# Attention probabilities scaled on GpSimd instead of VectorE and ScalarE, and six low-part splits moved the other way

## The chip, the core and the metric

The kernel runs on one core of one Trainium2 chip. A core has several engines with their own instruction streams: TensorE (PE in the profile; its weight loads are listed apart as PEld), VectorE (DVE), ScalarE (ACT), GpSimd (POOL) and SyncE (SP), which here issues loads. The engines work on SBUF, a memory of 128 partitions; matrix products land in PSUM banks and are read from there by VectorE and ScalarE. Each engine works through its own instructions in order and waits on semaphores for the others. DMAs are issued from the streams of SyncE and GpSimd, so an issue stands in line with that engine's other instructions.

The metric is the device time of one execution in microseconds. The kernel before took 1936.27 us, the median of three runs from 1935.07 to 1936.42.

## The reference

One layer of an encoder trunk over 1024 tokens of width 1024, all in float32:

```
h = x + 1/2 * SwiGLU_1(RMSNorm(x))
[qA|kA|vA|qB|kB|vB|gA|gB] = RMSNorm(h) @ W_in
yA = NeighbourhoodAttention2D(qA, kA, vA)      # 8 heads of 64, learned 2-D bias
yB = WindowedGQA(rope(qB), rope(kB), vB)       # 8 heads, 2 key heads, window 128, sink logit
h = h + (sigmoid(gA) * (yA @ W_A) + sigmoid(gB) * (yB @ W_B)) @ W_out
h = h + 1/2 * SwiGLU_2(RMSNorm(h))
y = RMSNorm(h)
```

The attention B has one learned sink logit for each head. It joins the denominator of the softmax without a value:

```
m = max(max(s), sink)
e = exp(s - m)
p = e / (sum(e) + exp(sink - m))
```

## The kernel before

**Precision.** Matrix products are taken with operands split in two: a high part, which is a copy rounded to the format `fp32r`, and a low part, the difference. The helper `split` does it: line 93 copies on ScalarE, line 94 subtracts on VectorE or on the engine given to it. A product then takes three passes, lines 145, 147 and 149 of the helper `mm3`. So L93, L94, L145, L147 and L149 in the profile belong to many callers, told apart by the tile (`ws` weights and probabilities, `ar` large resident operands, `fx` values, `raw` what a load brought).

**Stages.** First feed-forward, input projection, attention with the gate projections between, the branch products and the merge, second feed-forward, final norm. The change touches the attention stage alone, roughly 846 to 1118 us of the span.

**Units.** Attention is cut in 64 units. A unit is one block of 128 queries for two heads (s = 0, 1). Units 0 to 31 belong to attention B (8 query blocks, 4 head pairs each), units 32 to 63 to attention A (4 head pairs, 8 query blocks each). The first and last query block see two key blocks (256 columns), the others three (384 columns).

A unit passes three functions, each in a later turn of one loop:

- `scores(un)`: for each head, two matmuls into a PSUM bank `d` (L1278, L1279). For units of attention B a copy of the sink logit into column 0 of the tile's row (L1282). A fused instruction on VectorE adds the bias and finds the minimum of the negated scores, `nmx` (L1283). ScalarE takes the exponential and its sum, `ssum` (L1286). After both heads VectorE takes the reciprocals `rc` of the two sums (L1289) and scales head 0 (L1290); ScalarE scales head 1 (L1291). The probabilities lie in `fa`, in two buffers used in turn; `fa` also holds biases and the outputs of attention A.
- `turn(un)`: the probabilities are transposed by TensorE into PSUM (L1299) and split (L93 on ScalarE, L94 on VectorE) into `ws`.
- `values(un)`: products with the values (L1313, L1318), whose result goes to the output blocks (L1231, L1233, L1252, L1253, L1256) and from there to memory by a store from GpSimd's queue.

**The loop.** Turn n issues scores(n), then a step of filler work, turn(n−1), another step, values(n−2). The filler is a generator of matmul groups that do not depend on the units: the gate projections (L145, L147, L149 into `g`), at the end of the stage the products of branch B. At n = 23, 33, 41 and 49 `prep_a` prepares the next head pair of attention A: twelve loads issued from GpSimd (L1090, L1092), one more load, transposes of the values (L1104), and their splits into `fx`.

**Outputs y.** When the outputs of attention are complete they are read back from memory and split for the branch products: `split_y`, called for four blocks of B (two in the last gate step, two at the head of `branch_b`) and for three blocks of A (at n = 60, 61, 62). Six of the seven calls give GpSimd for the low part (L94, `ar` from `raw`, 128 x 1024); one of B's gives VectorE.

**What sets the order.** The program is written in the order above; a list scheduler then sets each engine's own order from the dependences and from when it expects results to be ready. A longer expected time on one engine can so move other instructions within TensorE's order.

Of the kernel before, what the change touches and what calls it, by code (L numbers as in the profile page):

```python
# [12 lines left out]
AF = mybir.ActivationFunctionType  # L13
ALU = mybir.AluOpType

P = 128
# [20 lines left out]
def trunk_kernel(ctx, tc, x, xt, n1, wg1, wu1, wd1, nm, win, rpb, sink, wa, wb, wo,  # L37
                 n2, wg2, wu2, wd2, nf, c_rope, c_mask_a, c_mask_b, out):
    nc = tc.nc
# [33 lines left out]
    def new_ar(g, dt=F32R):  # L73
        ar[g] = main.tile([P, 4, 1024], dt, tag=f"ar{g}", bufs=1, name=nm_("ar"))
        return ar[g]

    def slot(k):
        return ar[k // 4][:, k % 4, :]

    def bank(tag):  # L80
        return ps.tile([P, 512], F32, tag=tag, name=nm_(tag))
# [10 lines left out]
    def split(dst_hi, dst_lo, src, eng=None):  # L92
        nc.scalar.copy(dst_hi, src)  # L93
        (eng or nc.vector).tensor_tensor(dst_lo, src, f32v(dst_hi), op=ALU.subtract)  # L94
# [12 lines left out]
    def load_w(w, c0, r=None, eng=None):  # L107

        return load_split(ws4(), ws4(), w_cols(w, c0), w.shape[0] // P, P, r, eng)
# [41 lines left out]
    def drain(gen, n=1 << 30):  # L151

        for _ in range(n):
            if next(gen, gen) is gen:
                return
# [784 lines left out]
    def by_block(a):  # L940

        return a.rearrange("p (b j x) -> p j b x", b=NTT, x=16)

    def in_block(a):
        return a.rearrange("p (j b x) -> p j b x", b=NTT, x=16)
# [170 lines left out]
    def gate(dc, steps):  # L1116

        w = mix.pop("gate")
        bs = [bank("g"), bank("g")]
        for k, c in enumerate((4, 5, 6, 7, 0, 1, 2, 3)):  # L1120
            mm3(bs, k == 0, k == NC8 - 1, (w[0][:, c, :], w[1][:, c, :]), [u_half(c, n) for n in range(2)])
            yield
            if k in steps:
                steps[k]()
        gt = xs4()
        for n in range(2):
            nc.scalar.copy(gt[:, n * 512:(n + 1) * 512], bs[n])
        nc.gpsimd.dma_start(g_d[dc * P:(dc + 1) * P, :], gt)
# [5 lines left out]
    def branch_w(w, dc, eng=None, r=None):  # L1134

        t = ws4()
        if r is None:
            r = fetch_branch(raw4()[:, :512], w, dc)
        split(t[:, :512], t[:, 512:], r, eng)
        return [t[:, k:k + 512].rearrange("p (c f) -> p c f", f=P) for k in (0, 512)]  # L1140

    Y_A, Y_B = ((12, 13), (14, 15), (20, 21), (22, 23)), ((4, 5), (6, 7), (0, 1), (2, 3))

    def branch_mm(bs, w, y):

        for c in range(4):
            mm3(bs, c == 0, c == 3, (w[0][:, c, :], w[1][:, c, :]),
                [[slot(k)[:, n * 512:(n + 1) * 512] for k in y[c]] for n in range(2)])
            yield

    def fetch_y(r0):
        mix["y", r0] = raw4()
        nc.sync.dma_start(mix["y", r0], y_d[r0:r0 + P, :])

    def split_y(slots, r0, eng):

        h, l = [slot(k) for k in slots]
        r = mix.pop(("y", r0))
        if r0 < 512:
            r = in_block(r)  # L1160
            h, l = by_block(h), by_block(l)
        split(h, l, r, eng)
# [4 lines left out]
    def branch_a(i):  # L1167

        w = branch_w(wa[0], a_order[i], nc.gpsimd, a_raw.get(i))
        bs = [bank("gd"[i % 2]) for _ in range(2)]  # L1170
        a_mm.append((bs, branch_mm(bs, w, Y_A)))

    def merged(dc):
        return slot((16, 17, 18, 19, 24, 25, 26, 27)[dc])

    def gate_b(dc):
        rb = xs4()
        nc.sync.dma_start(rb, g_d[D + dc * P:D + (dc + 1) * P, :])
        nc.scalar.activation(rb, rb, AF.Sigmoid)
        return rb  # L1180

    def branch_b():

        for c in range(2, 4):
            split_y(Y_B[c], c * P, nc.vector if c == 2 else nc.gpsimd)
        for g in (4, 6):
            new_ar(g, F32)
        nxt = branch_w(wb[0], 0, nc.vector), gate_b(0)
        for dc in range(NC8):
            w, rb = nxt  # L1190
            bs = [bank("dg"[dc % 2]) for _ in range(2)]
            yield from branch_mm(bs, w, Y_B)
            if dc + 1 < NC8:
                nxt = branch_w(wb[0], dc + 1, nc.vector), gate_b(dc + 1)
            for n in range(2):
                sl = slice(n * 512, (n + 1) * 512)
                nc.vector.tensor_tensor(merged(dc)[:, sl], bs[n], rb[:, sl], op=ALU.mult)

    def filler():
        for dc, nxt in zip(gates, gates[1:] + [None]):  # L1200
            if nxt is not None:
                yield from gate(dc, {4: lambda: mix.update(gate=load_w(win[0], GA + nxt * P))})
            else:
                yield from gate(dc, {0: lambda: [fetch_y(c * P) for c in range(2)],
                                     4: lambda: [split_y(Y_B[c], c * P, nc.gpsimd) for c in range(2)],
                                     5: lambda: [fetch_y(c * P) for c in range(2, 4)]})
        yield from branch_b()
        for i in range(2):
            branch_a(i)
            for _ in range(3):  # L1210
                drain(a_mm[i][1], 1)
                yield

    fill = filler()
    nfill = len(gates) * 8 + 38


    def small(name, n=2):
        return main.tile([P, 2], F32, tag=name, bufs=n, name=nm_(name))
# [48 lines left out]
    def scores(un):  # L1268
        j = un["j"]
        k0, k1 = max(j - 1, 0), min(j + 2, NTT)  # L1270
        nw = (k1 - k0) * P
        moff = (k0 - j + 1) * P
        ext = 0 if un["sink"] is None else 1
        nmx, ssum, rc = small("nmx"), small("ssum"), small("rc")
        un.update(k0=k0, nk=k1 - k0, pr=[])
        for s in range(2):
            b = bank("d")
            nc.tensor.matmul(b[:, :nw], un["q"][s], un["kd"][s][:, k0 * P:k1 * P], start=True, stop=False)  # L1278
            nc.tensor.matmul(b[:, :nw], un["q"][s], un["kl"][s][:, k0 * P:k1 * P], start=False, stop=True)  # L1279
            pr = fa[:, 1536 + (2 * (npair[0] % 2) + s) * (384 + ext):][:, :ext + nw]  # L1280
            if ext:
                nc.vector.tensor_copy(pr[:, 0:1], un["sink"][s])  # L1282
            nc.vector.tensor_tensor_reduce(out=pr[:, ext:], in0=b[:, :nw], in1=un["bias"][s][:, moff:moff + nw], scale=-1.0,  # L1283
                                           scalar=un["sink"][s] if ext else BIG, op0=ALU.add, op1=ALU.min,
                                           accum_out=nmx[:, s:s + 1])
            nc.scalar.activation(pr, pr, AF.Exp, scale=-1.0, bias=nmx[:, s:s + 1], accum_out=ssum[:, s:s + 1])  # L1286
            un["pr"].append(pr[:, ext:])
        npair[0] += 1
        nc.vector.reciprocal(rc, ssum)  # L1289
        nc.vector.tensor_scalar_mul(un["pr"][0], un["pr"][0], rc[:, 0:1])  # L1290
        nc.scalar.activation(un["pr"][1], un["pr"][1], AF.Copy, scale=rc[:, 1:2])  # L1291

    def turn(un):
        nk = un["nk"]
# [30 lines left out]
    def filling(share):  # L1325
        nonlocal spent
        spent += rate * share
        drain(fill, int(spent))
        spent -= int(spent)
# [8 lines left out]
    for n in range(1 << 30):  # L1338
        got = next(source, None)
        if got is not None:  # L1340
            scores(got)
        pipe.insert(0, got)
        for hp, n0 in preps.items():
            if n == n0:
                prep = prep_a(hp)
        if prep:
            drain(prep, 1)
        filling(0.5)
        if len(pipe) > 1 and pipe[1] is not None:
            turn(pipe[1])  # L1350
        if prep:
            drain(prep, 1)
        if n in (58, 59, 61):
            fetch_y(512 + min(n - 58, 2) * P)
        if n in (60, 61, 62):
            split_y(Y_A[n - 60], 512 + (n - 60) * P, nc.gpsimd)
        filling(0.5)
        if len(pipe) > 2 and pipe[2] is not None:
            values(pipe[2])
        pipe = pipe[:3]  # L1360
        if not any(pipe):
            break
# [194 lines left out]
```

## Time and profile before

| | before |
|---|---|
| median of three runs | 1936.27 us |
| profiled execution, first to last instruction (span) | 1934.8 us |
| time of a run outside the span, median less span | 1.5 us |
| TensorE (PE) busy | 1922.2 us (99%) |
| VectorE (DVE) busy | 1437.1 us (74%) |
| ScalarE (ACT) busy | 943.6 us (49%) |
| GpSimd (POOL) busy | 295.5 us (15%) |
| attention stage, 846 to 1118 us: PE, DVE, ACT, POOL busy | 271.33, 232.39, 220.52, 51.65 of 272 us |

The profile is of one execution. A line of a timeline gives the start in us from the beginning of the span, the duration, the engine, the line, the operation, the tiles out<-in with the shape, the count of instructions joined in it, and in brackets how long the engine had sat idle before and what it waited for. A line of groups gives busy us and the mean ns of one, and behind the bar the idle time before them with the releaser. A line of waits gives who waited, for whom, us in total, times, and the longest. Matmuls are pipelined: the shown duration of one matmul is longer than the step to the next.

### The profile page before, as it was taken

What the parts mean: (1) busy time and instruction counts of PE and PEld (TensorE: products, weight loads), DVE (VectorE), ACT (ScalarE), POOL (GpSimd) and SP (SyncE); (2) the same over time, 40 slices, a digit from 0 to 9 for tenths busy, and PEclk for the clock granted to TensorE, in tenths of its full rate; (3) what the DMA queues carried; (4) which work ended last, traced back from release to release, by engine and by line L of the source; (5) the groups of instructions that cost most, each with busy time, mean ns of one, the idle gap of its engine ahead of it and who ended that gap; (6) DMA issues with size and microseconds to landing.
All of it is one profiled execution on the core that took longest, in us unless ns stands there. A gap on an engine that the chain in (4) does not pass through costs nothing.

```text
span 1934.8 us, 25499 instructions
## 1 busy us (share of the span) xinstructions
PE 1922.2 (99%) x8956; PEld 1603.1 (83%) x8956; DVE 1437.1 (74%) x2560; ACT 943.6 (49%) x1827; POOL 295.5 (15%) x432
## 2 busy tenths in 40 slices
PE   9999999999999999999999999999999999999998
PEld 7888888888888888888888888878888888888886
DVE  7987765668957788678888857889676566569864
ACT  6532333344446543477877862365333333344453
POOL 0011110013300112211122231010111001005210
PEclk9999999999999999999999999999999999999999
DMA  6344323286234478553458576533423323493341
GB/s 261 100 167 163 129 104 128 86 289 225 88 109 137 159 223 250 185 163 104 116 134 195 184 242 210 169 140 133 147 87 109 126 87 109 140 355 104 112 144 61
DMA packets 151745, 298.70 MB, mean 154 GB/s; under 512 B 14912, under 2 KB 64448, under 8 KB 151616
## 3 DMA queue, kind: packets, MB, share of 16 engines
q1 hardware_dynamic: 123072, 210.53, 33.6%
q0 software_dynamic: 27824, 85.48, 13.3%
q8 instruction: 71, 1.16, 0.3%
q10 hardware_dynamic: 720, 1.05, 0.1%
q14 instruction: 58, 0.48, 0.1%
HBM read 210.50 MB, written 88.27 MB: 154 GB/s over the span
## 4 chain that ended last, share of the span: by engine, by line
PE 88%; issue 7%; POOL 1%; DMA 1%; DVE 1%; ACT 1%; POOLq 0%; SPq 0%; ACTq 0%; DVEq 0%
PE g L149 16%; PE g L147 16%; PE g L145 16%; PE d L149 11%; PE d L147 11%; PE d L145 11%; PE d L1299 2%; PE g L1313 1%; PE g L1318 1%; PE d L1278 1%; PE d L1279 1%; POOL zs_d L889 1%; PE d L138 1%; POOL z_d L891 1%; DMA zr_d<-xs 0%
## 5 line engine op out<-in xcount | busy, mean ns | idle before, releaser
L145 PE MATMUL g<-ar,ws 128*128 128x512 f32 x1128 | 423.1, 395 | 0.6 <-ACT fa L911 0.6
L147 PE MATMUL g<-ar,ws 128*128 128x512 f32 x1128 | 417.2, 390 | 0.9 <-DVE ar L94 0.5
L149 PE MATMUL g<-ar,ws 128*128 128x512 f32 x1128 | 416.1, 390 | 0.2 <-DVE ws L311 0.2
L145 PE MATMUL d<-ar,ws 128*128 128x512 f32 x736 | 282.4, 391 | 0.3 <-ACT ar L810 0.2
L147 PE MATMUL d<-ar,ws 128*128 128x512 f32 x736 | 281.9, 390 | 0.3 <-DVE ar L812 0.3
L149 PE MATMUL d<-ar,ws 128*128 128x512 f32 x736 | 281.6, 390 | 0.5 <-DVE ws L311 0.5
L147 PEld LDWEIGHTS g<-ar,ws 128*128 128x128 f32 x1128 | 211.8, 188 | 46.2 <-DVE ar L94 1.0
L149 PEld LDWEIGHTS g<-ar,ws 128*128 128x128 f32 x1128 | 211.7, 188 | 45.5 <-DVE ws L311 0.7
L145 PEld LDWEIGHTS g<-ar,ws 128*128 128x128 f32 x1128 | 206.4, 188 | 37.8 <-ACT fa L911 1.0
L311 DVE TENSOR_TENSOR ws<-raw,ws 128x512 fp32r<-128x512 f32 x204 | 139.6, 690 | 99.6 <-ACT ws L308 98.8
L308 ACT CAST ws<-raw 128x512 fp32r<-128x512 f32 x204 | 125.1, 620 | 140.6 <-PE g L149 64.4
L145 PEld LDWEIGHTS d<-ar,ws 128*128 128x128 f32 x736 | 138.3, 188 | 29.7 <-ACT ar L810 0.6
L147 PEld LDWEIGHTS d<-ar,ws 128*128 128x128 f32 x736 | 138.4, 188 | 29.6 <-DVE ar L812 0.6
L149 PEld LDWEIGHTS d<-ar,ws 128*128 128x128 f32 x736 | 138.4, 188 | 29.4 <-DVE ws L311 0.7
L93 ACT CAST ws<-raw 128x512 fp32r<-128x512 f32 (+1 forms) x121 | 81.0, 669 | 144.0 <-PE d L149 61.8
L94 DVE TENSOR_TENSOR ws<-raw,ws 128x512 fp32r<-128x512 f32 (+1 forms) x119 | 93.7, 789 | 59.8 <-ACT ws L93 59.3
L414 POOL DMA_DIRECT2D hid<-fx x91 | 49.3, 542 | 431.5 <-DVE fx L474 304.9
L93 ACT CAST ar<-raw 128x512 fp32r<-128x512 f32 (+1 forms) x83 | 56.0, 679 | 94.8 <-PE g L147 55.0
L94 DVE TENSOR_TENSOR ws<-ar,ws 128x512 fp32r<-128x512 f32 x114 | 98.3, 867 | 3.8 <-ACT ws L93 3.7
L145 PE MATMUL g<-ws,ws 128*128 128x512 f32 x232 | 91.0, 392 | 0.0
L149 PE MATMUL g<-ws,ws 128*128 128x512 f32 x232 | 90.5, 390 | 0.0
L147 PE MATMUL g<-ws,ws 128*128 128x512 f32 x232 | 90.3, 389 | 0.0
(313 smaller groups left out, 3607.4 us busy)
## 6 DMA issues: line engine op xcount, KB each, us to landing
raw<-hid SPq DMA_DIRECT2D x70, 512.0 KB
hid<-fx POOLq DMA_DIRECT2D x91, 256.0 KB, 2.4
ar<-in_ffn_w_down_dram SPq DMA_DIRECT2D x32, 512.0 KB
raw<-in_ffn_w_up_dram SPq DMA_DIRECT2D x31, 512.0 KB
raw<-in_ffn_w_gate_dram SPq DMA_DIRECT2D x27, 512.0 KB
raw<-in_w_in_dram SPq DMA_DIRECT2D x27, 512.0 KB
hid<-fa POOLq DMA_DIRECT2D x51, 256.0 KB, 2.7
ar<-zs_d POOLq DMA_DIRECT2D x48, 256.0 KB, 5.3
```

What stands on the lines that cost most here:

```text
L93: nc.scalar.copy(dst_hi, src)
L94: (eng or nc.vector).tensor_tensor(dst_lo, src, f32v(dst_hi), op=ALU.subtract)
L138: nc.tensor.transpose(pt[:, c * P:(c + 1) * P], xs[:, (half * 4 + c) * P:(half * 4 + c + 1) * P], ident)
L145: nc.tensor.matmul(b, lhs[0], r[0], start=first, stop=False, **kw)
L147: nc.tensor.matmul(b, lhs[0], r[1], start=False, stop=False, **kw)
L149: nc.tensor.matmul(b, lhs[1], r[0], start=False, stop=last, **kw)
L308: nc.scalar.copy(w[0][:, :512], a)
L311: nc.vector.tensor_tensor(w[0][:, 512:], a, f32v(w[0][:, :512]), op=ALU.subtract)
L414: nc.gpsimd.dma_start(hid[PRODUCTS.index(p), i], src)
L889: nc.gpsimd.dma_start(d[ch * P:(ch + 1) * P, cols], t)
L891: nc.gpsimd.dma_start(z_d[ch * P:(ch + 1) * P, cols], c)
L1299: nc.tensor.transpose(pt[:, i * P:(i + 1) * P], un["pr"][s][:, i * P:(i + 1) * P], ident)
```

## The change

Three edits, all in the attention stage:

1. The copies of the sink logit (L1282, 64 of 128 x 1) run on GpSimd instead of VectorE.
2. Both scalings by the reciprocal of the sum (64 on VectorE at L1290, 64 on ScalarE at L1291) become 128 tensor-scalar multiplications on GpSimd, head 0 and then head 1 of each unit.
3. The six low parts of the outputs y that GpSimd computed (L94, 128 x 1024) are computed by VectorE.

What is computed stays the same.

```diff
@@ branch_b
-            split_y(Y_B[c], c * P, nc.vector if c == 2 else nc.gpsimd)
+            split_y(Y_B[c], c * P, nc.vector)
@@ filler
-                                     4: lambda: [split_y(Y_B[c], c * P, nc.gpsimd) for c in range(2)],
+                                     4: lambda: [split_y(Y_B[c], c * P, nc.vector) for c in range(2)],
@@ scores
             if ext:
-                nc.vector.tensor_copy(pr[:, 0:1], un["sink"][s])
+                nc.gpsimd.tensor_copy(pr[:, 0:1], un["sink"][s])
...
         nc.vector.reciprocal(rc, ssum)
-        nc.vector.tensor_scalar_mul(un["pr"][0], un["pr"][0], rc[:, 0:1])
-        nc.scalar.activation(un["pr"][1], un["pr"][1], AF.Copy, scale=rc[:, 1:2])
+        for s in range(2):
+            nc.gpsimd.tensor_scalar(un["pr"][s], un["pr"][s], rc[:, s:s + 1], None, op0=ALU.mult)
@@ the loop over units
         if n in (60, 61, 62):
-            split_y(Y_A[n - 60], 512 + (n - 60) * P, nc.gpsimd)
+            split_y(Y_A[n - 60], 512 + (n - 60) * P, nc.vector)
```

## The prediction

> **What bounds the kernel now.** I read the page's first part, then busy time by stage, then the waits of the attention stage (the only place where edited lines run), then the timeline of single units.
>
> ```profile
> PE 1922.2 (99%) x8956; PEld 1603.1 (83%) x8956; DVE 1437.1 (74%) x2560; ACT 943.6 (49%) x1827; POOL 295.5 (15%) x432
> ```
>
> TensorE is the bound of the whole program. The stage of the edited lines runs from 846 to 1118 us; the second row below is its last part, after which other work follows. The columns are the length, then the busy us and the instructions of each engine.
>
> ```profile
> core 0: us, PE busy (x) PEld busy (x) DVE busy (x) ACT busy (x) POOL busy (x), PEclk, DMA share, GB/s
> 846.00:1118.00 272.00, 271.33 (x1605) 238.29 (x1605) 232.39 (x767) 220.52 (x567) 51.65 (x79) 1.00 0.55 145
> 1080.00:1120.00 40.00, 40.00 (x241) 35.18 (x240) 34.33 (x107) 35.61 (x86) 13.37 (x9) 1.00 0.56 193
> ```
>
> PE idles 0.67 us of 272 here, at clock 1.00: the most that any change in this stage can win without removing matmuls is near nothing. DVE and ACT are busy 85% and 81%, POOL 19%. So I do not ask which engine gets lighter, but whether each unit's probabilities still reach PE in time. The waits of PE on the edited chain, in the stretch 838 to 1130:
>
> ```profile
> PEld g L147 <- DVE ar L94: 1.0, 1, 1.0
> PEld d L1299 <- ACT fa L1291: 0.6, 3, 0.2
> ```
>
> The first stands at the start of the stage:
>
> ```profile
> 844.84 0.15 DVE L1282 COPY fa<-nsk 128x1 f32<-128x1 f32 x1 [3.78 <-DMA z_d<-fa]
> ...
> 848.67 1.23 DVE L94 TENSOR_TENSOR ar<-raw,ar 128x1024 fp32r<-128x1024 f32 x1
> ...
> 849.95 0.50 PE L147 MATMUL g<-ar,ws 128*128 128x512 f32 x1 [0.53 <-DVE ar L94]
> ```
>
> A sink copy, in DVE's queue, waits 3.78 us for a store out of the same tile `fa`; three splits behind it run late, and PE waits for the last of them. Counting also the lengthened matmul starts around it, PE loses about 0.8 us (an estimate from the 1.0 and 0.53 of these rows), and some 0.5 at the three waits on L1291.
>
> A normal unit, number 20 of 64:
>
> ```profile
> 930.25 0.34 PE L1279 MATMUL d<-ar,ar 128*128 128x384 f32 x1
> 932.42 0.63 ACT L1286 ACTIVATE fa<-fa,nmx 128x385 f32<-128x385 f32 x1
> 933.17 0.17 DVE L1289 RECIPROCAL rc<-ssum 128x2 f32<-128x2 f32 x1
> 933.38 0.42 DVE L1290 TENSOR_SCALAR fa<-fa,rc 128x384 f32<-128x384 f32 x1
> 933.97 0.62 ACT L1291 ACTIVATE fa<-fa,rc 128x384 f32<-128x384 f32 x1
> 935.28 0.82 PE L1299 MATMUL d<-ident,fa 128*128 128x128 f32 x6
> ```
>
> Scores end at 930.59, the reciprocal at 933.34 (2.75 us later), the transposes begin 1.9 us after that; between them PE runs gate matmuls. The new chain must fit into this gap. The tightest units have much less, at both ends of the stage:
>
> ```profile
> 849.81 0.16 DVE L1289 RECIPROCAL rc<-ssum 128x2 f32<-128x2 f32 x1
> 850.75 0.49 PE L1299 MATMUL d<-ident,fa 128*128 128x128 f32 x3
> ```
>
> ```profile
> 1102.03 0.33 PE L1279 MATMUL d<-ar,ar 128*128 128x384 f32 x1
> ...
> 1106.23 0.17 DVE L1289 RECIPROCAL rc<-ssum 128x2 f32<-128x2 f32 x1
> ...
> 1107.03 0.82 PE L1299 MATMUL d<-ident,fa 128*128 128x128 f32 x6
> ```
>
> These are units 0 and 60, the first and last of nine (0, 2, 11, 31, 40, 55, 56, 57, 60) whose first transposes' weights load 0.5 to 1.0 us after the reciprocal (for units 0 and 60, about 0.55).
>
> **The change part by part.** Rows for the costs:
>
> ```profile
> L1290 DVE TENSOR_SCALAR fa<-fa,rc x64: 336/420/966, 850.0 to 1117.7; 128x384 f32<-128x384 f32 x48, 128x256 f32<-128x256 f32 x16
> ```
>
> ```profile
> L1291 ACT ACTIVATE fa<-fa,rc x64: 495/620/641, 850.0 to 1117.8; 128x384 f32<-128x384 f32 x48, 128x256 f32<-128x256 f32 x16
> ```
>
> ```profile
> L1282 DVE COPY fa<-nsk x64: 131/144/155, 838.9 to 973.0; 128x1 f32<-128x1 f32 x64
> ```
>
> ```profile
> L126 POOL TENSOR_SCALAR st<-st x20: 222/223/1270, 582.8 to 1881.0; 128x1 f32<-128x1 f32 x20
> ```
>
> ```profile
> L94 POOL TENSOR_TENSOR ws<-ar,ws 128x512 fp32r<-128x512 f32 x6 | 7.7, 1291 | 19.0 <-ACT ws L93 19.0
> ...
> L94 POOL TENSOR_TENSOR ar<-raw,ar 128x1024 fp32r<-128x1024 f32 x6 | 14.8, 2464 | 22.0 <-ACT ar L93 22.0
> ```
>
> ```profile
> L94 DVE TENSOR_TENSOR ws<-raw,ws 128x1024 fp32r<-128x1024 f32 x13 | 15.9, 1224 | 3.4 <-ACT ws L93 3.2
> ...
> L1073 DVE TENSOR_TENSOR fa<-raw,masks 128x384 f32<-128x384 f32 x16 | 8.5, 550 | 0.1
> ```
>
> Engine time: DVE loses 64 x 0.42 + 64 x 0.144 = 36 us and gains 6 x 1.22 = 7 us. ACT loses 64 x 0.62 = 38 us (at most: 16 of its instructions are shorter). POOL loses 6 x 2.46 = 15 us and gains 128 scalings and 64 copies. PE needs none of this busy time; it hides under PE's 99%.
>
> *Price of a scaling on POOL.* No row shows a one-input elementwise instruction of POOL on 384 columns. Below stands 0.42 us, what DVE takes for the same shape. Above stands POOL's two-input rate: (2.46 − 1.29)/512 = 2.3 ns a column, with 0.22 for the smallest instruction: 0.22 + 384 x 2.3 ns = 1.1 us. With one input instead of two it should lie between: I take 0.75, the middle (0.57 for 256 columns at that rate). The 128 of them with 64 copies at 0.22 to 0.3 make some 105 us, so POOL stands near 50% busy.
>
> The Trainium skill's "GPSIMD Engine Reference", section "Engine selection", says that two-input elementwise work is about twice as slow on GpSimd as on VectorE but one-input work runs roughly at line rate. This trace agrees on the first half (2.46 against 1.22 us); no row shows the second. By it a scaling would cost near 0.55 us (an estimate), and the sum below would shrink to that of the first rival.
>
> *Chain from reciprocal to transposes.* Before: two engines in parallel, 0.5 to 1.2 us, as unit 20 shows. After: two scalings in sequence on POOL, 1.5 us, and about 0.1 for the hand-over (in unit 20 the reciprocal starts 0.12 after the exponential on ACT ends). The first head's transposes need 0.1 + 0.75 = 0.85 us; the second head's come 0.37 later (half of the six 128-column passes in 0.82), so the whole pair needs about 1.25 (0.9 with 256 columns). A unit with 1.9 hides it. A tight one falls short by (need − gap).
> - Units 0, 2, 11, 31, 40, with gaps of 0.55, 0.83, 1.00, 0.51 and 0.89, miss 0.37, 0.09, 0.25, 0.41, 0.03. DVE's queue ahead of the reciprocal is shorter there by copies and an earlier scaling (0.56 us), so I keep under half: **+0.5**.
> - Units 55, 56, 57, 60, with 0.86, 0.69, 1.01 and 0.57, miss 0.06, 0.23, 0.24, 0.68: 1.2. The six splits of 1.22 us join DVE exactly here, where it is already busy 34.3 of 40 us. Each can sit in front of a reciprocal; I add 0.8 for two of them: **+2.0**.
>
> *Order of PE's work.* In the built program most transposes keep their place in PE's order. Around the third and fourth preparation of heads, units 42, 43 and 50, 51 are turned one to three filler steps later. Counted in PE passes at the trace's durations, from a unit's scores to its transposes lie 6.2 us before and 9.7 after for unit 42, but 6.8 and 3.8 for unit 44; 6.2 and 12.0 for unit 50, but 5.5 and 3.5 for unit 52. Four units' transposes then follow at 2.9, 2.4, 3.3 us.
> A unit needs 2.4 to 3.4 us to its reciprocal (unit 20: 2.75) and 1.25 beyond, some 4.6 in a loaded stretch. Unit 44 misses 0.8 and unit 52 1.1. DVE needs (232.4 − 36 + 7)/64 = 3.2 us a unit, so steps of 2.9 and 2.4 miss up to 0.3 and 0.8; further 0.5 and 1.1 for both bunches, as splits of the prepared values run there too: **+1.3** and **+2.2**.
>
> *Sink copies.* The wait of 3.78 us leaves DVE's queue and goes to POOL's. Behind it on POOL stand small copies and stores whose readers come much later. DVE's three splits start earlier, PE's loss goes: **−0.8**. Later on POOL's copies are not urgent, since the next exponential waits longer for the bias and minimum on DVE. Without that cover one costs some 0.1 us (0.22 by L126 against 0.144).
>
> *Splits to VectorE.* Removing 2.46 us instructions from POOL keeps scalings from queueing behind them; the low parts come 1.2 us sooner, and nothing waits for them.
>
> *POOL's DMA queue.* The preparation's loads go through POOL, and some wait for scores:
>
> ```profile
> POOL ar L1090 <- PE d L1279: 15.2, 5, 6.2
> ```
>
> With scalings behind such a load, a 6.2 us wait could hold up a unit. In the new order the load that waits for scores of unit 47 has unit 46's scalings behind it. Its scores come before those transposes; between 0 and 1 us, taken at 0, as unit 46's gap of scores to transposes is 5.3 us.
>
> *Shared port.* A scaling of POOL reads SBUF while DVE runs two-input instructions out of SBUF:
>
> ```profile
> 509.37 0.68 DVE L94 TENSOR_TENSOR ws<-raw,ws 128x512 fp32r<-128x512 f32 x1
> 509.60 1.61 POOL L565 TENSOR_TENSOR ar<-ar,ar 128x512 f32<-128x512 f32 x1 [1.42 <-DVE ar L562]
> 509.98 1.78 DVE L94 TENSOR_TENSOR ws<-ar,ws 128x512 fp32r<-128x512 f32 x1
> ```
>
> The same DVE instruction takes 0.68 alone and 1.78 beside POOL, and POOL 1.61 instead of 1.29. In this stage such DVE instructions are the 13 of 1.22, the 16 of 0.55 and the six new ones; the bulk of DVE's work reads PSUM. About 35 meetings of up to 0.75 us each fall mostly in gaps of 1.9 us: 0 to 3 us, taken at 0 beside the 0.8 above. The Trainium skill's "SBUF — State Buffer" calls this pair an exclusive lock, in which the later instruction fully blocks; the 1.78 agrees with it.
>
> **Sum.** −0.8 + 0.5 + 1.3 + 2.2 + 2.0 = +5.2 us. The span of 1934.8 and 1.5 us around it make the median of 1936.27; the forecast is 1936.3 + 5.2 = **1941.5 us**, slower by 0.27%. I call 0.2% (3.9 us) the least that differs from no change.
>
> **Rivals.**
> 1. *Cover holds.* At a scaling of 0.5 us the pair needs 0.8 us after the reciprocal. The nine tight units then miss nothing much, DVE's lighter queue (a sixth of its stage time) absorbs the bunches, and PE stalls only some 1 to 2 us around units 44 and 52. With −0.8: 1936 to 1938, say 1937. For it: DVE's 36 us of relief. Against: no POOL row at such a rate.
> 2. *POOL at its two-input rate, with port meetings.* At 1.1 us a pair ends 2.3 us after the reciprocal, and normal units with 1.9 (and the 0.37 of grace) sit on the edge; any meeting on the port makes PE wait. Thirty units at 0.3 us, nine tight ones at 0.7 more, bunches at 1.5 times: 9 + 4.2 + 5.3 − 0.8 = +14 to +18, about 1952. For it: the only wide POOL rows.
> 3. *Faster.* If DVE and ACT, lighter by 29 and 38 us, let every reciprocal come 0.5 us sooner, and a scaling costs at most 0.55, the 0.8 at the start and the 0.5 at L1291 go and nothing comes: 1936.3 − 1.3 = 1935.0. It cannot reach 0.2%, since PE's idle time in the stage is under 1 us.
>
> **How the numbers follow.** Forecast (stalls of 2.5 to 10 us): 0.51, of which 0.10 lies under 3.9 us; cover holds: 0.27; two-input rate: 0.17; faster: 0.05, of which 0.03 could exceed 0.2% by something unseen. So faster 0.03, same 0.27 + 0.10 + 0.02 = 0.39, slower 0.41 + 0.17 = 0.58. Range: 1935.4 takes in most of the covered cases, 1951 half of the second rival; the likeliest case's own range is 1938.5 to 1946.
>
> **What would show it.** Right: L1291 on POOL at 0.65 to 0.85 us for 384 columns; PE waits "L1299 <- POOL L1291" at nine tight units and near units 44 and 52, in all 4 to 8 us; the wait at 849.95 gone; DVE near 204 us in the stage. Wrong: L1291 on POOL at 0.5 or 1.1; L1299 waits at ordinary units; DVE L94 from SBUF stretched beyond 2 us and PE waiting for its `ws`; a load of L1090 in POOL's queue with a scaling stuck behind it.

## The result and the profile after

The changed kernel takes 1960.57 us (median of four runs, 1959.63 to 1961.65), the kernel before 1936.35 us beside it: 24.2 us slower, a ratio of 1.0127 with a 95% interval of 1.0115 to 1.014. The forecast was 1941.5 us, its range ended at 1951.

The page's first part and the attention stage after, which now ends near 1142 instead of 1118 us:

```profile
PE 1929.3 (98%) x8956; PEld 1601.2 (82%) x8956; DVE 1417.2 (72%) x2438; ACT 913.9 (47%) x1763; POOL 446.3 (23%) x618
```

```profile
core 0: us, PE busy (x) PEld busy (x) DVE busy (x) ACT busy (x) POOL busy (x), PEclk, DMA share, GB/s
846.00:1142.00 296.00, 279.79 (x1610) 237.86 (x1609) 211.92 (x644) 191.26 (x503) 204.88 (x263) 1.00 0.49 134
```

TensorE's idle time in the stage went from 0.67 us in 272 to 16.2 us in 296, at the same clock. The other 8 us are in its busy time, which is modelled and also covers a matmul that starts late. VectorE and ScalarE are lighter by 21 and 29 us (29 and at most 38 were forecast); GpSimd is busy 69%, more than the half that was forecast. The lines of the new scalings and the waits on them (stretch 838 to 1160 us):

```profile
L1291 POOL TENSOR_SCALAR fa<-fa,rc 128x384 f32<-128x384 f32 x96 | 120.3, 1263 | 46.7 <-DVE rc L1289 36.7 <-DVE fx L94 2.9 <-PE d L1279 2.1
L1291 POOL TENSOR_SCALAR fa<-fa,rc 128x256 f32<-128x256 f32 x32 | 32.3, 1018 | 14.5 <-DVE rc L1289 12.3 <-PE d L1279 1.7 <-POOL fa L1282 0.2
```

```profile
POOL fa L1291 <- DVE rc L1289: 49.1, 28, 6.1
...
PEld d L1299 <- POOL fa L1291: 29.1, 44, 1.5
...
PE d L1299 <- POOL fa L1291: 16.7, 32, 1.3
```

A scaling of 384 columns takes 1.26 us on average where 0.75 was taken, above even the upper bound of 1.1. The transposes wait for it 44 times (the PEld row; the PE row tells of the same waits), where before they waited three times on L1291. Of the 16.7 us of the PE row 15.4 lie in the stage: nearly all of TensorE's idle time there. GpSimd itself waits 49 us for reciprocals, so it isn't short of time: it is late after each reciprocal.

Unit 20 after, the unit that the prediction showed:

```profile
937.04 0.17 DVE L1289 RECIPROCAL rc<-ssum 128x2 f32<-128x2 f32 x1
...
937.37 2.47 POOL L1291 TENSOR_SCALAR fa<-fa,rc 128x384 f32<-128x384 f32 x2
...
939.18 0.49 PE L1299 MATMUL d<-ident,fa 128*128 128x128 f32 x3
...
939.89 0.55 PE L1299 MATMUL d<-ident,fa 128*128 128x128 f32 x3 [0.23 <-POOL fa L1291]
```

From the reciprocal's end to the end of the second scaling 2.6 us pass, where before both engines were done 1.25 us after it. The first head's transposes still find their data; the second head's do not, and PE waits. So an ordinary unit with 1.9 us of cover, not only the nine tight ones, is now late.

### The profile page after: what moved, and what is told of

Its sections match the earlier page's. It is cut to its first block, busy times and chain, and to the rows that moved or that the text cites. A ratio compares the mean times of both kernels' runs of the same rounds, so it can differ in the third digit from the quotient of the medians.

```text
span 1959.1 us, 25864 instructions
## 1 busy us (share of the span) xinstructions
PE 1929.3 (98%) x8956; PEld 1601.2 (82%) x8956; DVE 1417.2 (72%) x2438; ACT 913.9 (47%) x1763; POOL 446.3 (23%) x618
## 4 chain that ended last, share of the span: by engine, by line
PE 49%; POOL 3%; DVE 2%; issue 2%; ACT 2%; POOLq 0%; DVEq 0%; ACTq 0%
PE g L149 9%; PE g L147 9%; PE g L145 9%; PE d L149 6%; PE d L145 6%; PE d L147 6%; POOL fa L1291 3%; PE d L1299 2%; PE g L1318 1%; PE g L1313 1%; ACT fa L1286 1%; PE d L1278 1%; PE d L1279 1%; ACT ws L93 0%; DVE ws L94 0%
## 5 line engine op out<-in xcount | busy, mean ns | idle before, releaser
L147 PE MATMUL g<-ar,ws 128*128 128x512 f32 x1128 | 417.2, 390 | 0.4 <-DVE ar L833 0.4
L147 PE MATMUL d<-ar,ws 128*128 128x512 f32 x736 | 281.4, 389 | 0.3 <-DVE ar L812 0.3
L147 PEld LDWEIGHTS g<-ar,ws 128*128 128x128 f32 x1128 | 211.6, 188 | 44.7 <-DVE ar L833 0.8
L1291 POOL TENSOR_SCALAR fa<-fa,rc 128x384 f32<-128x384 f32 (+1 forms) x128 | 152.6, 1201 | 61.2 <-DVE rc L1289 49.1
L147 PEld LDWEIGHTS d<-ar,ws 128*128 128x128 f32 x736 | 138.2, 188 | 29.3 <-DVE ar L812 0.9
L94 DVE TENSOR_TENSOR ws<-raw,ws 128x512 fp32r<-128x512 f32 (+1 forms) x119 | 93.3, 786 | 58.6 <-ACT ws L93 58.3
L94 DVE TENSOR_TENSOR ws<-ar,ws 128x512 fp32r<-128x512 f32 x114 | 98.2, 867 | 5.5 <-ACT ws L93 5.5
L1286 ACT ACTIVATE fa<-fa,nmx 128x385 f32<-128x385 f32 (+3 forms) x128 | 75.5, 590 | 44.1 <-DVE nmx L1283 40.7
L94 DVE TENSOR_TENSOR ar<-raw,ar 128x512 fp32r<-128x512 f32 (+1 forms) x83 | 64.9, 785 | 36.8 <-ACT ar L93 35.5
```

The costliest lines, as they stand in the source:

```text
L147: nc.tensor.matmul(b, lhs[0], r[1], start=False, stop=False, **kw)
L1291: nc.gpsimd.tensor_scalar(un["pr"][s], un["pr"][s], rc[:, s:s + 1], None, op0=ALU.mult)
```

## The experiments

### One part at a time

Only the sink copies (e1), only the splits (e2), only the scalings (e3) are changed against the kernel before:

```diff
 e1
-                nc.vector.tensor_copy(pr[:, 0:1], un["sink"][s])
+                nc.gpsimd.tensor_copy(pr[:, 0:1], un["sink"][s])
 e2 (and likewise the other five blocks)
-            split_y(Y_A[n - 60], 512 + (n - 60) * P, nc.gpsimd)
+            split_y(Y_A[n - 60], 512 + (n - 60) * P, nc.vector)
 e3
-        nc.vector.tensor_scalar_mul(un["pr"][0], un["pr"][0], rc[:, 0:1])
-        nc.scalar.activation(un["pr"][1], un["pr"][1], AF.Copy, scale=rc[:, 1:2])
+        for s in range(2):
+            nc.gpsimd.tensor_scalar(un["pr"][s], un["pr"][s], rc[:, s:s + 1], None, op0=ALU.mult)
```

> Only the sink copies (L1282) go to GpSimd; scalings and splits as before. Theory 'every part but the scalings is nearly free': the wait at the start of the stage (849.95, DVE ar L94 late) shrinks, 1935.3 to 1936.3 us, ratio 0.9994 to 1.0. Rival 'the copies take part in the loss' (POOL's copies wait for ScalarE, 21.3 us in 26 waits in the changed kernel, and hold up the exponential): 1937 us or more.

> Only the six low parts of y (split_y) go to VectorE. Theory 'nearly free': 1935.5 to 1937 us. Rival 'the six splits crowd VectorE at the end of the stage' (the changed kernel loses 6.4 us over units 55 to 63): 1938 to 1942 us.

> Only the two scalings of each unit go to GpSimd. Theory 'the scalings make the loss': 1958 to 1962 us, as the changed kernel. Rival 'the splits or the copies carry a good part': 1954 us or less; if the six splits of 2.46 us left on GpSimd now stand in front of scalings, 1962 to 1968 us.

Measured: e1 1936.53 us (ratio 1.0001, 0.9993 to 1.001), e2 1937.25 us (1.0006, 0.9997 to 1.0015), e3 1962.71 us (1.0137, 1.0123 to 1.015). Each lies a little above the range that was expected, by 0.2, 0.25 and 0.7 us, which is less than the width of its interval. The scalings alone make the whole loss. e3 touches the rival of 1962 to 1968 us (splits left on GpSimd ahead of scalings), but its 2 us above the changed kernel are within the intervals. In e1 the row "PEld g L147 <- DVE ar L94: 1.0, 1, 1.0" of the kernel before is no longer among the waits, and GpSimd has the long wait instead (stretch 838 to 1130 us):

```profile
POOL fa L1282 <- ACT fa L1286: 59.2, 47, 3.7
...
POOL fa L1282 <- DMA z_d<-fa: 3.1, 1, 3.1
...
ACT fa L1286 <- POOL fa L1282: 0.4, 1, 0.4
```

GpSimd's copies wait 59 us for ScalarE, yet ScalarE waits for them only 0.4 us: that wait costs nothing. The stall that went is under 1 us, less than these runs can tell from nothing.

### The price of a scaling

The changed kernel, with each scaling cut to a half (e4) or three quarters (e10) of its columns; the other columns stay unscaled. The edit of e4 (e10 has `nw * 3 // 4` in place of `nw // 2`):

```diff
-            nc.gpsimd.tensor_scalar(un["pr"][s], un["pr"][s], rc[:, s:s + 1], None, op0=ALU.mult)
+            nc.gpsimd.tensor_scalar(un["pr"][s][:, :nw // 2], un["pr"][s][:, :nw // 2], rc[:, s:s + 1], None, op0=ALU.mult)
```

> The changed kernel with each scaling on only the first half of its columns (192 of 384, 128 of 256); the second halves stay unscaled. By the changed kernel's 1.245 us for 384 and 0.92 for 256 columns a scaling then takes about 0.76 us, the price that the prediction took, and TensorE's order stays nearly that of the changed kernel (units 42, 43, 50, 51 still turned late). Theory 'the loss is the price of the scalings': the prediction's sum of +5 us holds, 1938 to 1944 us. Rival 'the loss is the moved order and does not depend on the price': 12 us or more stay, 1948 us and up.

> The changed kernel with each scaling on three quarters of its columns (288 of 384, 192 of 256); the last quarters stay unscaled. By 2.5 ns a column a scaling takes 1.0 us (0.78). Theory 'threshold': an ordinary unit has about 1.9 us after the reciprocal, and 0.2 + 2 x 1.0 - 0.4 = 1.8 still fits, so only the units turned after a late one lose: 1941 to 1946 us. Rival 'in proportion to the price' between +2.7 at 0.76 us and +24 at 1.245: about 1950 us.

Measured: e4 1938.89 us (1.0017, 1.0008 to 1.0027), e10 1949.21 us (1.0066, 1.0052 to 1.008). The lines of the scalings of three-block units and the waits on the scalings, first in e4, then in e10:

```profile
L1291 POOL TENSOR_SCALAR fa<-fa,rc 128x192 f32<-128x192 f32 x96 | 73.7, 776 | 59.1 <-DVE rc L1289 49.1 <-PE d L1279 3.6 <-PE g L1313 2.7
```

```profile
PEld d L1299 <- POOL fa L1291: 5.5, 12, 1.2
```

```profile
L1291 POOL TENSOR_SCALAR fa<-fa,rc 128x288 f32<-128x288 f32 x96 | 98.0, 1030 | 50.3 <-DVE rc L1289 42.1 <-PE g L1313 2.8 <-PE d L1279 1.9
```

```profile
PEld d L1299 <- POOL fa L1291: 14.5, 26, 1.5
```

With 0.78, 1.03 and 1.26 us a scaling, the loss is 2.7, 12.8 and 24.2 us, and the transposes wait 12, 26 and 44 times. At the price that the prediction took, the time is 1938.9, within the likeliest case's range. The theory of a threshold at 1.9 us fell: the loss grows with the price at all three points. The reading that fits is that the covers of the units are spread, so that each 0.1 us of price pushes further units over theirs. Between these three points a 0.1 us costs 4 to 5 us of the total, about a third of the 12.8 us that 128 scalings would take if none were hidden.

### Where the price comes from

A dozen GpSimd instructions are added at the head of the kernel before, where GpSimd has little other work. The edit, with the four of the kind that the change uses (scalings by a constant, copies and two-input products follow):

```diff
     fa = main.tile([P, 4096], F32, name="fa")
+    nc.gpsimd.memset(fa[:, :1024], 1.0)
+    for w_ in (128, 256, 384, 768): nc.gpsimd.tensor_scalar(fa[:, :w_], fa[:, :w_], nhalf, None, op0=ALU.mult)
```

> The kernel before with a dozen GpSimd instructions at its very start, where GpSimd has nothing to do: scalings in place by a column of scalars on 128, 256, 384 and 768 columns, the same by a constant, copies and two-input products on 128 and 384. Theory 'GpSimd's own speed': the scaling of 384 takes 1.2 to 1.25 us here too, 2.5 ns a column. Rival 'the shared port with VectorE': 0.5 to 0.8 us here.

The run was taken once; only its profile is used. The first row groups the four scalings (shortest, median, longest), the others are single ones. VectorE's first instruction in this run starts at 5.74 us, after the three shorter ones:

```profile
L68 POOL TENSOR_SCALAR fa<-fa,nhalf x4: 618/1090/2207, 2.2 to 5.3; 128x128 f32<-128x128 f32 x1, 128x256 f32<-128x256 f32 x1, 128x384 f32<-128x384 f32 x1, 128x768 f32<-128x768 f32 x1
```

```profile
2.19 0.62 POOL L68 TENSOR_SCALAR fa<-fa,nhalf 128x128 f32<-128x128 f32 x1
...
2.90 0.94 POOL L68 TENSOR_SCALAR fa<-fa,nhalf 128x256 f32<-128x256 f32 x1
```

```profile
3.93 1.24 POOL L68 TENSOR_SCALAR fa<-fa,nhalf 128x384 f32<-128x384 f32 x1
```

So 1.24 us is GpSimd's own speed, with VectorE still idle: about 0.3 us and 2.4 ns a column by these three. (The other instructions ran while VectorE was at work and give no clean price; even so the copy of 384 columns took 0.85 us.) Against that the changed kernel's mean of 1.263 leaves 0.02 us a scaling for meetings with VectorE on the shared port; that rival is out as the cause of the price. VectorE's two-input splits of `raw` into `ws` (13 of 128 x 1024), which could lose by such meetings, take 1.270 us on average after, 1.224 before.

A few meetings do count. The second scaling of unit 63, the last, starts at about 1142.5 while one of the splits that the change moved to VectorE is running:

```profile
1141.60 2.67 POOL L1291 TENSOR_SCALAR fa<-fa,rc 128x256 f32<-128x256 f32 x2 [2.17 <-DVE rc L1289]
...
1142.26 1.22 DVE L94 TENSOR_TENSOR ar<-raw,ar 128x1024 fp32r<-128x1024 f32 x1
...
1144.33 0.44 PE L1299 MATMUL d<-ident,fa 128*128 128x128 f32 x2 [1.31 <-POOL fa L1291]
```

The first scaling of this pair takes 0.92 us, the second 1.77, and PE waits 1.31 us. Both scalings of unit 55 are longer in the same way, by 0.75 and 0.64 us, beside two-input work of L1073. From these three I estimate 1 to 2 of the 24.2 us.

### Where the loss sits, and two remedies

For each unit I took the start of the second head's transposes in the profiled run less that in the kernel before (us; a run's profile can sit about 1 to 2 us off another's before the stage begins):

```
unit                 0    10    20    30    41    49    54    58    63
changed kernel     -0.5   0.5   4.4   5.6   7.2  11.2  18.6  21.6  25.0
e4_half            -1.6  -1.9  -1.1  -0.9  -0.6  -0.6   1.6   1.9   2.9
e5_spread          -1.0  -0.1   3.8   5.7   7.1  10.1  11.9  13.6  16.6
e6_later           -0.5  -2.2  -0.2  -0.5  -0.8  -0.1   3.2   8.1  11.4
e9_later_spread     0.9  -0.8   1.2   0.9   0.5   0.5   1.1   1.5   2.6
```

In the changed kernel the first 42 units lose 7.7 us in steps below 2 us; units 42 to 54 lose 11.4, and the end 6.4. The steepest part comes with the fourth preparation of heads, at n = 49. Units 50 to 52 after:

```profile
1070.80 2.13 POOL L1090 DMA_DIRECT2D ar<-zs_d  x4
...
1071.89 0.17 DVE L1289 RECIPROCAL rc<-ssum 128x2 f32<-128x2 f32 x1
1072.88 1.08 POOL L1092 DMA_DIRECT2D ar<-zs_d  x2
1073.90 0.64 POOL L1259 DMA_DIRECT2D y_d<-fa  x1
1074.54 4.93 POOL L1291 TENSOR_SCALAR fa<-fa,rc 128x384 f32<-128x384 f32 x4
...
1081.00 0.82 PE L1299 MATMUL d<-ident,fa 128*128 128x128 f32 x6
...
1084.09 0.83 PE L1299 MATMUL d<-ident,fa 128*128 128x128 f32 x6
...
1085.79 0.17 DVE L1289 RECIPROCAL rc<-ssum 128x2 f32<-128x2 f32 x1
...
1086.14 2.47 POOL L1291 TENSOR_SCALAR fa<-fa,rc 128x384 f32<-128x384 f32 x2 [6.12 <-DVE rc L1289]
...
1087.44 0.55 PE L1299 MATMUL d<-ident,fa 128*128 128x128 f32 x3 [0.77 <-POOL fa L1291]
...
1088.66 0.55 PE L1299 MATMUL d<-ident,fa 128*128 128x128 f32 x3 [0.68 <-POOL fa L1291]
```

The reciprocal of unit 50 is done at 1072.1, but six loads and a store are ahead of the scalings in the queue, three of the loads and the store still to be issued; the scalings begin 2.5 us later. TensorE doesn't wait for that: the row groups the scalings of units 50 and 51, which end at 1079.5, and the transposes of unit 50 come only at 1081, with no wait in their row. TensorE's order puts them there. Unit 51 follows 3 us behind, again without a wait. Units 52 to 57 then have too little between scores and transposes: nothing stands between the reciprocal of unit 52 and its scalings, and PE waits 0.77 and 0.68 us for them. Over units 52 to 57 PE waits 7.3 us in this way, more than two fifths of its 16.7.

Two remedies were tried on the changed kernel, apart and together. e5 spreads the loads of one head pair over more steps. With that the built program also turns units 42, 43, 50 and 51 at their old place in TensorE's order:

```diff
                 for a in halves(dst[k]):
                     nc.gpsimd.dma_start(a, head(k, 4, lo))
+                yield
```

> The changed kernel with the twelve GpSimd loads of prep_a issued in six steps of two (the yield inside the loop) instead of two steps of six. In the built program units 42, 43, 50 and 51 are then turned at their old place in TensorE's order (scores to transposes 5.0 to 6.4 us of passes), the scalings keep their price. Theory 'the late turns make the bunches': the jumps of the changed kernel at units 42 to 54 (about 11 us together) and some of the lockstep after them go, 1945 to 1951 us. Rival 'the price alone': 1956 us or more.

e6 puts all filler of a turn ahead of the transposes, e9 has both:

```diff
-        filling(0.5)
+        filling(1.0)
         if len(pipe) > 1 and pipe[1] is not None:
             turn(pipe[1])
...
-        filling(0.5)
         if len(pipe) > 2 and pipe[2] is not None:
             values(pipe[2])
```

> The changed kernel with both filler shares of a loop turn issued ahead of the transposes (filling 1.0, then 0) instead of half before and half after. Where two steps fall in a turn, scores to transposes grows by 1.39 us of TensorE passes; the late turns of units 42, 43, 50, 51 stay in the order. Theory 'latency': the chain of two scalings in sequence, 2.5 us, is only late, and more work ahead of the transposes covers it: the 7 us of units 0 to 41 go and part of the end's 6, 1944 to 1950 us. Rival 'rate': GpSimd's queue cannot deliver a unit in 4.25 us (two scalings, loads and stores), then 1956 us or more.

> The changed kernel with both remedies: all filler of a turn ahead of the transposes, and the preparation's loads spread, so that no unit is turned late. Theory 'latency': with 5.9 to 7.8 us of TensorE passes between scores and transposes nearly every unit covers 2.7 + 0.2 + 2.5 - 0.4 = 5.0 us, 1936.5 to 1941 us. Rival 'a second cause at the end' (the lockstep of units 54 to 63, where 8 us were lost even with the later transposes): 1943 to 1946 us.

Measured: e5 1953.19 us (1.0085, 1.007 to 1.01), a little above what was expected; e6 1945.83 us (1.0048, 1.0031 to 1.0065); e9 1936.06 us (1.0, 0.9991 to 1.0009), a little below. Beside the kernel before, the loss is 16.6, 9.2 and −0.3 us instead of 24.2: the spread is worth 7.6, the later transposes 15, both together all of it. In e9 a scaling still takes its 1.25 us and GpSimd is busy 204 us in the stage; but TensorE hardly waits for it:

```profile
L1291 POOL TENSOR_SCALAR fa<-fa,rc 128x384 f32<-128x384 f32 x96 | 118.8, 1246 | 31.1 <-DVE rc L1289 18.1 <-PE d L1299 6.8 <-PE d L1279 2.3
```

```profile
PEld d L1299 <- POOL fa L1291: 3.2, 6, 0.7
```

So in the main neither GpSimd's rate nor contention made the loss, but latency: two scalings in sequence between a reciprocal and transposes that TensorE's order had put too close. Whether e5 gains by the loads' place in GpSimd's queue or by TensorE's order, no run takes apart; the waits above speak for the order. The unit table shows both remedies at work where they should be: e5 removes most of the jump after unit 49 and leaves the first 42 units alone, e6 removes the loss of the first 50 and leaves most of the rest.

The end (units 54 to 63) loses 6 to 8 us in the changed kernel and in e6, but 1.5 in e9. There one unit begins only when the one before is through. Units 53 and 54 of the changed kernel:

```profile
1091.19 2.47 POOL L1291 TENSOR_SCALAR fa<-fa,rc 128x384 f32<-128x384 f32 x2 [2.58 <-DVE rc L1289]
...
1092.20 0.07 DVE L1283 DVE_READ_ACCUMULATOR2_ANT nmx<- 128x1 f32 x1
...
1093.71 0.55 PE L1299 MATMUL d<-ident,fa 128*128 128x128 f32 x3 [0.68 <-POOL fa L1291]
...
1094.35 0.48 ACT L93 CAST ws<-d 128x384 fp32r<-128x384 f32 x1 [0.74 <-PE d L1299]
...
1094.73 0.62 ACT L1286 ACTIVATE fa<-fa,nmx 128x384 f32<-128x384 f32 x1
```

Unit 54's minimum is there at 1092.3, but its exponential begins at 1094.73, because in ScalarE's queue it stands behind the high-part copy of unit 53's transposes, which wait for the scaling. A late unit so delays the next one through ScalarE's order. This is read from the trace; no run changes that order alone.

### Only one scaling on GpSimd, and two versions meant to be faster

e7 is the changed kernel with head 0 back on VectorE; e11 the same with both remedies; e12 the kernel before with the sink copies on GpSimd and the later transposes.

```diff
-        for s in range(2):
-            nc.gpsimd.tensor_scalar(un["pr"][s], un["pr"][s], rc[:, s:s + 1], None, op0=ALU.mult)
+        nc.vector.tensor_scalar_mul(un["pr"][0], un["pr"][0], rc[:, 0:1])
+        nc.gpsimd.tensor_scalar(un["pr"][1], un["pr"][1], rc[:, 1:2], None, op0=ALU.mult)
```

> The changed kernel with head 0 scaled by VectorE again and only head 1 by GpSimd: the two scalings run side by side, 1.4 us instead of 2.7 after the reciprocal. Theory 'the sequence of two is what is late': an ordinary unit has 1.9 us and covers it, 1936 to 1941 us. Rival 'each scaling on GpSimd costs its share': half the loss, about 1948 us.

> As the run with both remedies, but head 0 scaled by VectorE again. If the attention stage then makes TensorE wait nowhere, the time is that of the kernel before less its 1.3 us of waits there: 1934.5 to 1936 us, ratio 0.999 to 1.0. If it is above 1937 us, the remedies themselves cost.

> The kernel before with the sink copies on GpSimd and all filler of a turn ahead of the transposes; scalings and splits as before. TensorE's waits of 1.3 us in the stage go: 1934.5 to 1936 us, ratio 0.999 to 1.0. If it is above 1937 us, the later transposes make values or buffers late.

Measured: e7 1936.24 us (0.9999, 0.9989 to 1.0008), e11 1934.99 us (0.9995, 0.9986 to 1.0004), e12 1938.5 us (1.001, 1.0001 to 1.0019). One scaling on GpSimd costs nothing though it lasts as long: it runs beside the other, and the pair is done 1.57 us after the reciprocal in most units of three blocks, instead of 2.6. It isn't the engine but the sequence of two that is too long. e7 keeps the loads in sixes and the late turns of units 50 and 51, so these cost nothing either where the chain is short. No version is measurably faster than the kernel before; with TensorE idle 0.67 us in the stage there was nothing left to win. e12 was expected at 1934.5 to 1936 us and is slightly worse than the kernel before; its waits name a place that had 0.3 us there:

```profile
PEld g L145 <- ACT xs L1127: 3.4, 4, 1.5
PE g L145 <- ACT xs L1127: 1.9, 2, 1.0
```

The gate matmuls wait for ScalarE to empty their PSUM banks, while ScalarE still does half of the scalings there. That this makes the 2 us isn't shown.

## Why the prediction was wrong, point by point

**What bounds the kernel.** Right. The question was whether probabilities reach TensorE in time, not which engine is lighter; VectorE and ScalarE lost 21 and 29 us of work in the stage and nothing was won by it.

**Price of a scaling on POOL: the step that failed.** The middle of 0.42 and 1.1 us was taken, 0.75; measured 1.24 alone and 1.26 in place. The choice of the middle rested on "with one input instead of two it should lie between", for which no row stood. The upper end was too low as well: the smallest instruction was taken for the fixed part (0.22, measured about 0.3) and the slope of two-input work, 2.3 ns, for the worst (measured 2.4 with one input). With it the need of a pair was too small: the whole chain is done 2.6 us after the reciprocal and not 1.6, so ordinary units, which the sum left out, make TensorE wait. The Trainium skill's "GPSIMD Engine Reference", section "Engine selection", has one-input work at roughly line rate. This case doesn't agree: 0.55 us was the estimate by it, 1.24 is measured, three times VectorE's 0.42.

**The rest of the sum, at its own price.** e4 tests it: +2.7 us (1.5 to 5.2 by its interval) where +5.2 was summed. So at that price the time is about as forecast, but the terms are only in part right: by the unit table of e4 nothing is lost at units 42 to 49 (+1.3 in the sum), 2.2 from 49 to 54 (+2.2), 1.3 at the end (+2.0).

**Order of PE's work.** Right as a place for the second bunch: the jump at unit 50 and after is the largest of the trace, and in e5, which has no late turns, most of it goes. At the true price e5 wins 7.6 us, where the sum had 3.5 for both bunches; the spread loads have a part in it that isn't known. The chain from this place to the end, unit after unit through ScalarE's queue, was not foreseen.

**Sink copies and splits.** Right in size, as far as the runs can tell: the stall at 849.95 is gone, and both parts alone are within 0.1% of the kernel before. The −0.8 for the copies and the +0.8 for the splits are too small for these runs to show. In the changed kernel one of the moved splits lengthened the last scaling.

**POOL's DMA queue.** The delay was larger than the 0 to 1 us considered, its cost was 0 as taken. It wasn't a wait of a load that held scalings up, but the issue itself, 0.5 to 0.6 us for each load or store: unit 50's scalings begin 2.5 us after its reciprocal, but its transposes come later still and wait for nothing.

**Shared port.** Taken at 0. The scalings are longer in place than alone by 96 x 0.02 + 32 x 0.08 = 4.5 us in all, of 152.6. The meetings of units 55 and 63 fall where TensorE waits and cost an estimated 1 to 2 us.

**Rivals.** The second, with its mechanism of ordinary units on the edge, is what happened, though without much of its port meetings. Its 1952 us was worked out at 1.1 us; between 1949.2 at 1.03 and 1960.6 at 1.26 the runs give about 1953 there. That they agree is in part luck: nine tight units at 0.7 us are 6.3 us, and its sum has 4.2. The price it was given was too low; at the measured one its sum of stalls would have had to be half as large again.

## What to carry to other kernels

Where the receiving engine has no row for an instruction like the one moved to it, the middle of two bounds is a guess. Here the nearest row, two-input work, gave 1.1 us and was much closer to the 1.24 than the middle: "one input instead of two" was worth nothing for this scaling. When work leaves two engines that ran side by side and goes in sequence to one, count the latency of the sequence against the cover of an ordinary unit, and look whether what stands ahead of it in the new engine's queue, DMA issues included, makes a consumer wait. If such a chain is too long but the engine has time to spare, more independent work ahead of the consumer can hide it: in e9, together with the spread loads, it hid all of it.

## What was not expected of the hardware

A scaling with one SBUF input and a column of scalars costs GpSimd 2.4 ns a column, no less than its two-input instructions (2.3 ns by the rows of the kernel before). And VectorE's scaling, which also reads one SBUF operand, and one on GpSimd that runs beside it slow each other, depending on which starts first: in e7

```profile
933.81 0.42 DVE L1290 TENSOR_SCALAR fa<-fa,rc 128x384 f32<-128x384 f32 x1
933.94 1.40 POOL L1291 TENSOR_SCALAR fa<-fa,rc 128x384 f32<-128x384 f32 x1
...
937.56 1.24 POOL L1291 TENSOR_SCALAR fa<-fa,rc 128x384 f32<-128x384 f32 x1 [0.20 <-DVE rc L1289]
937.99 0.41 DVE L1290 TENSOR_SCALAR fa<-fa,rc 128x384 f32<-128x384 f32 x1
...
1003.26 1.24 POOL L1291 TENSOR_SCALAR fa<-fa,rc 128x384 f32<-128x384 f32 x1 [4.43 <-DVE rc L1289]
1003.45 0.61 DVE L1290 TENSOR_SCALAR fa<-fa,rc 128x384 f32<-128x384 f32 x1
```

GpSimd takes 1.40 us where VectorE was already running, and 1.24 where GpSimd was first; in the 30 units of three blocks where VectorE led by 0.07 to 0.17 us, GpSimd took 1.37 to 1.47. In the third pair GpSimd led by 0.19 us and VectorE's scaling took 0.61 instead of 0.42: it was held up, but done 0.79 us after GpSimd's start, well before GpSimd's end. With a lead of 0.43 us, as in the second pair, neither was longer. Whether that is the same port as in the two-input meetings isn't shown.
